# The first product of a squared-ReLU MLP in matmuls of 256 columns, added in PSUM, and a shift of the token tiles

## The chip, the cores and the metric

The kernel runs on one core of a Trainium2 chip. The metric is the device time of one execution in microseconds (us), as the median of several runs. A profile of one execution gives the times of single instructions; it names the engines PE (TensorE, the matmuls), PEld (TensorE's weight loads), ACT (ScalarE), DVE (VectorE), POOL (GpSimd) and SP (SyncE, which issues the loads). "L521" is line 521 of the kernel that the profile belongs to.

## The reference

A trunk of two layers on 256 tokens of 2048 floats. The first layer mixes tokens by a convolution module, the second by latent attention; each is followed by an MLP of width 8192, and a norm stands ahead of every part. The MLP is the part that matters here:

```python
def sq_relu_mlp(h, w1, w2):
    return jnp.square(jax.nn.relu(h @ w1)) @ w2

for layer in range(DEPTH):
    ...
    h = rms_norm(x, norm_mlp_g[layer])
    x = x + sq_relu_mlp(h, mlp_w1[layer], mlp_w2[layer])
return rms_norm(x, final_norm_g)
```

Here x is 256 x 2048, w1 2048 x 8192 and w2 8192 x 2048, all in float32.

## The kernel before, in words

**Products in three terms.** TensorE multiplies in a rounded format (float32r). A float32 matrix `a` is therefore split into `hi` (rounded) and `lo` (the rest), and a product `a b` is taken as hi·hi + hi·lo + lo·hi. ScalarE writes `hi` and VectorE the difference `lo` (`split_into`, lines 431 and 432). In down products `mm3` (L200 to L202) issues the three matmuls, each of 512 columns.

**Tokens.** The normed tokens stand transposed in four tiles `xt`, made by `open_xt`. Each holds four of the 16 slices k of 128 input channels; a slice is 256 floats `xh` (hi of the 256 tokens), and right behind it 256 floats `xl` (lo). `xhl(k)` takes both as one operand of 512 columns. The tiles are written by transposes on TensorE (L256, `to_T`), by `residual_stage` for what follows.

**The first product of the MLP**, `h @ w1`, is cut into up units of 128 of the 8192 inner channels: a load of 1 MB of w1 and two chunks of eight slices. The weights are the stationary operand, the tokens stream. Chunk 0 issues eight matmuls of hi weights on `xhl` (512 columns: hi·hi in the left half of the PSUM tile, hi·lo in the right half; L521), then eight of low weights on `xh` (256 columns into the left half; L519); chunk 1 the low ones first. So a unit is 16 wide and 16 narrow matmuls, into one PSUM tile of 512 columns, which ScalarE copies into the tile `U` (L526). Of every two units, `add` puts the two halves together on VectorE (L538), `square` takes the maximum with 0 and the square on ScalarE (L543, then L546 or L549), `forms` (from L555) and `part` (L431, L432) make the operands of the second product. These steps wait in the list `todo`, and `stream` takes one or two of them whenever it prepares a chunk's weights, six chunks (`WB`) ahead of the chunk that TensorE runs.

**The second product** is cut into down units, each for a 1 MB piece of w2. In the first three quarters seven of eight use a scheme of seven instead of eight products (S) and one is plain (O), in the last fewer use it; either ends in matmuls of 512 columns from `mm3`.

**Order.** `mlp` goes through four quarters of the inner channels. First come the 16 up units of the first quarter; from then on the up units of the next quarter (T) and the down units of the present one alternate, by the strings of `ORDERS` (L57), and the last quarter's down units end the MLP. With the T that opens the first string, the first 17 up units of a layer follow each other; the other 47 stand in 42 rows of one or two, each row behind a down unit's wide matmuls.

**Other users of the same tiles and lines.** The conv layer (L864 to L866) and two projections in attention (L1453 to L1455, L1476 to L1478) issue their three terms as three matmuls of 256 columns. The conv layer uses `xt` with the tokens' places as they are given by `PAD_XT`. The low weights of up units stand 56 floats into a tile that `LO_GAP` makes 64 floats wider.

Of the kernel before, what the change touches and what calls it, by code (L numbers as in the profile page):

```python
# [10 lines left out]
F32 = mybir.dt.float32  # L11
# [4 lines left out]
ALU = mybir.AluOpType  # L16
# [23 lines left out]
PAD_RIGHT = 40  # L40
LO_GAP = 64
PAD_XT = 16
PAD_KV = 48
# [13 lines left out]
ORDERS = "STSTSTOSTSTSTSTT", "TSTSTSTOSTSTSTST"  # L57
N_S, N_G = 9, 2
SEVENS = tuple(((0, 1, 3, 4, 5, 6, 7),) * 3 + (last,) for last in ((0, 2, 4), (0, 2)))
# [28 lines left out]
def trunk_kernel(  # L88
# [230 lines left out]

    def open_xt(name, pad=0):  # L320
        pool = right_pool(name, 1)
        xt[:] = [
            pool.tile([P, KC // NNB, 2 * S], F32R, name=nm("xt")) for _ in range(NNB)
        ]
        if pad:
            pool.tile([P, pad], F32, name=nm("pad_xt"))

    xhl = lambda k: xt[k // 4][:, k % 4, :]
    xh = lambda k: xhl(k)[:, :S]
    xl = lambda k: xhl(k)[:, S:]  # L330
    open_xt("xtc", PAD_XT)
    spare = []
# [3 lines left out]

    def residual_stage(last, gain, r_scale=None):


        ssq = small.tile([P, T, NNB], F32, tag="ssq", name=nm("ssq"), bufs=2) if last else None  # L340

        def add(n, ps, t):
            sl = slice(n * NB, (n + 1) * NB)
            if r_scale is None:
                nc.vector.tensor_tensor(xs[:, t, sl], ps[t], xs[:, t, sl], op=ALU.add)
            else:
                nc.vector.scalar_tensor_tensor(
                    out=xs[:, t, sl], in0=ps[t], scalar=r_scale[:, t : t + 1], in1=xs[:, t, sl],
                    op0=ALU.mult, op1=ALU.add,
                )  # L350

        def prepare(n, only=None):
            sl = slice(n * NB, (n + 1) * NB)
            if last:
                if gain is not None:
                    for j in range(2):
                        to_T(xs, 4 * n + 2 * j, xh, xl, gain)
                for t in range(T) if only is None else [only]:
                    nc.scalar.activation(spare[-1](), xs[:, t, sl], AF.Square, accum_out=ssq[:, t, n : n + 1])

        return ssq, add, prepare
# [62 lines left out]

    def hi_lo(n, at=0):
        hi = wpool.tile([P, n, NB], F32R, tag="hi", name=nm("hi"), bufs=WB)
        lo = wpool.tile([P, n * NB + LO_GAP], F32R, tag="lo", name=nm("lo"), bufs=WB)
        return [hi, lo[:, at : at + n * NB].rearrange("p (a b) -> p a b", b=NB)]

# [55 lines left out]
    def mlp(layer, ssq, next_gain, finish=None, before=None, last_w1=None):  # L485
# [5 lines left out]
        def u_tile():  # L491
            return first_tiles.pop("u", None) or mp.tile([P, 2, 2 * S], F32, tag="U", name=nm("U"), bufs=2)

# [3 lines left out]
        def up_units(hs, q, p, extra):  # L497
# [5 lines left out]
            def up_unit(b):  # L503
                ps = []

                def chunk(h):
                    def prep(raw, parts):
                        parts[h] = [a.rearrange("p a (j n) -> p (a j) n", n=P) for a in hi_lo(2, LO_GAP - 8)]
                        split_into(parts[h], raw[:, 8 * h : 8 * h + 8, :])

                    def run(parts):
                        if not ps:
                            ps.append(acc_tile())
                        wh, wl = parts.pop(h)
                        for low in (h, 1 - h):
                            for j in range(8):
                                k = 8 * h + j
                                if low:
                                    nc.tensor.matmul(ps[0][:, :S], wl[:, j, :], xh(k), start=False, stop=False)  # L519
                                else:  # L520
                                    nc.tensor.matmul(ps[0], wh[:, j, :], xhl(k), start=k == 0, stop=k == KC - 1)  # L521

                    def out():
                        if b == 0:
                            held["u"] = u_tile()
                        nc.scalar.activation(held["u"][:, b, :], ps[0], AF.Copy)  # L526

                    if h == 0:
                        return Chunk(prep, run)
                    return Chunk(prep, run, [add, lambda: None, square, forms, part] + extra if b == 1 else [], now=out)  # L530

# [3 lines left out]

            def add():
                v = held["u"][:, :, :S]
                nc.vector.tensor_tensor(v, v, held["u"][:, :, S:], op=ALU.add)  # L538

            def square():  # L540
                n_s[0] += large
                v = held["u"][:, :, :S]
                nc.scalar.activation(v, v, AF.Relu)  # L543
                if p in sevens:
# [26 lines left out]
        def down_units(hs, q, n2, held, final):  # L571
# [5 lines left out]
            if last and not made_stage:  # L577
                made_stage.append(residual_stage(True, next_gain, r2))
            nssq, _, prepare = made_stage[0] if last else (None, None, None)
# [703 lines left out]

    ssq, due = mlp(0, ssq, g_mix[1])


    with ExitStack() as cx:
# [447 lines left out]

        open_xt("xt1")
        ssq, add, prepare = residual_stage(True, g_mlp[1])
        for b in range(2):
# [82 lines left out]
```

## Time and profile before

| | |
|---|---|
| timed runs | 1928.03 us median of 3 (1927.92 to 1928.38) |
| profiled execution, from the first to the last instruction | 1926.2 us, about 1.8 us less than the median |
| mean granted TensorE clock | 0.999 |
| instructions | 28463, of which 10768 matmuls |
| read from HBM, written | 363.68 MB, 2.10 MB (190 GB/s over the span) |
| up units, first MLP | from about 314 us on, mixed with down units from 403 us on |
| up units, second MLP | from about 1245 us on, mixed from 1334 us on |

How to read it: busy time of an engine is the sum of its instructions without their overlaps. Since matmuls are pipelined, the duration of one (0.28 us for 256 columns) is longer than the distance to the next one's start, and it is this distance that adds up. A row of a group ends with the mean duration in ns, then the idle time of the engine just ahead of these instructions and what ended most of it. A row of the timeline has start, duration, engine, line, operation, out<-in, shape and number; x8 is eight in a row. A row of the chain has start, duration and what ran.

### The profile page before, as it was taken

The page shows a single profiled execution, that of the slowest core. Times are in us where ns is not written, and L with a number is a line of the kernel's source. Part 1 is how long each engine was busy: PE and PEld are TensorE (multiplying, and loading weights), DVE is VectorE, ACT ScalarE, POOL GpSimd, SP SyncE. Part 2 cuts the span into 40 slices and gives each one's busy share as a digit, 9 for nine tenths or more (in the row PEclk, how much of TensorE's full clock was granted, in tenths as well). Part 3 has the DMA queues.
Part 4 walks back from the last instruction along what each step waited for, and adds up shares of the span by engine and source line. Part 5 has one row for each costly group of instructions (what it writes and reads, how often), then busy time and mean ns, then how long its engine had stood idle before and what let it go on. Part 6 is the DMA issues. An engine that isn't in the chain of part 4 may idle for free.

```text
span 1926.2 us, 28463 instructions
## 1 busy us (share of the span) xinstructions
PE 1900.7 (99%) x10768; PEld 1665.0 (86%) x10768; DVE 1648.4 (86%) x2370; ACT 1206.5 (63%) x1716; POOL 224.6 (12%) x185
## 2 busy tenths in 40 slices
PE   7999999999999999999999999999999999999998
PEld 7999888888888888888899998888888888888886
DVE  5999866789999999999976665667999999999887
ACT  5556754766666666666566665566666666666654
POOL 5999300000000000000001410000000000000000
PEclk9999999999999999999999999999999999999999
DMA  8676456857666677666646445765667666666663
GB/s 236 188 194 180 139 191 160 234 174 209 206 198 201 193 210 211 200 204 204 207 150 180 117 145 178 208 183 175 198 196 212 204 197 198 217 203 196 212 220 109
DMA packets 407114, 367.62 MB, mean 191 GB/s; under 512 B 15417, under 2 KB 351937, under 8 KB 406721
## 3 DMA queue, kind: packets, MB, share of 16 engines
q1 hardware_dynamic: 405952, 363.63, 63.1%
q10 hardware_dynamic: 1024, 2.17, 0.3%
q8 instruction: 84, 1.38, 0.3%
q14 instruction: 54, 0.43, 0.1%
HBM read 363.68 MB, written 2.10 MB: 190 GB/s over the span
## 4 chain that ended last, share of the span: by engine, by line
PE 88%; DVE 8%; ACT 2%; POOL 1%; issue 1%; DMA 1%; DVEq 0%; ACTq 0%; POOLq 0%
PE acc L521 24%; PE acc L201 15%; PE acc L200 15%; PE acc L202 15%; PE acc L519 12%; DVE sum L979 6%; POOL lo L175 1%; PE acc L256 1%; ACT hi L174 1%; PE acc L866 0%; PE acc L865 0%; PE acc L864 0%; PE acc L1589 0%; DMA xs<-in_x 0%; PE acc L1453 0%
## 5 line engine op out<-in xcount | busy, mean ns | idle before, releaser
L432 DVE TENSOR_TENSOR lo<-raw,hi 128x1024 fp32r<-128x1024 f32 (+1 forms) x512 | 570.6, 1121 | 88.1 <-ACT hi L431 87.8
L431 ACT ACTIVATE hi<-raw 128x1024 fp32r<-128x1024 f32 (+1 forms) x512 | 479.6, 970 | 66.3 <-PE acc L201 66.0
L521 PE MATMUL acc<-xt,hi 128*128 128x512 f32 x2048 | 504.3, 391 | 0.0
L521 PEld LDWEIGHTS acc<-xt,hi 128*128 128x128 f32 x2048 | 374.8, 188 | 73.0 <-ACT hi L431 0.4
L200 PE MATMUL acc<-hi,sh 128*128 128x512 f32 x930 | 362.8, 390 | 0.0
L202 PE MATMUL acc<-lo,sh 128*128 128x512 f32 x930 | 361.9, 389 | 0.0
L201 PE MATMUL acc<-hi,sl 128*128 128x512 f32 x802 | 312.0, 389 | 0.0
L519 PEld LDWEIGHTS acc<-xt,lo 128*128 128x128 f32 x2048 | 257.7, 188 | 10.9
L519 PE MATMUL acc<-xt,lo 128*128 128x256 f32 x2048 | 259.7, 279 | 0.0
L174 ACT ACTIVATE hi<-raw 128x1024 fp32r<-128x1024 f32 (+2 forms) x184 | 179.9, 1006 | 47.2 <-PE acc L201 43.0
L202 PEld LDWEIGHTS acc<-lo,sh 128*128 128x128 f32 x930 | 174.6, 188 | 36.3
L200 PEld LDWEIGHTS acc<-hi,sh 128*128 128x128 f32 x930 | 174.6, 188 | 36.0
L175 DVE TENSOR_TENSOR lo<-raw,hi 128x1024 fp32r<-128x1024 f32 (+2 forms) x118 | 132.8, 1145 | 68.6 <-ACT hi L174 62.5
L431 ACT ACTIVATE hi<-V 128x1024 fp32r<-128x1024 f32 x94 | 99.5, 1059 | 130.1 <-DVE V L727 117.4
L201 PEld LDWEIGHTS acc<-hi,sl 128*128 128x128 f32 x802 | 150.5, 188 | 31.2
L979 DVE SCALAR_TENSOR_TENSOR sum<-ub,w_dw,sum 128x256 f32<-128x256 f32 x392 | 158.9, 480 | 6.4 <-ACT sum L935 5.4
L175 POOL TENSOR_TENSOR lo<-raw,hi 128x1024 fp32r<-128x1024 f32 x66 | 157.6, 2406 | 23.1 <-ACT hi L174 22.5
L431 ACT ACTIVATE hi<-T 128x1024 fp32r<-128x1024 f32 x94 | 99.3, 1056 | 92.3 <-DVE T L715 70.5
L526 ACT ACTIVATE U<-acc 128x512 f32<-128x512 f32 x128 | 75.8, 592 | 110.4 <-PE acc L521 110.4
L864 PE MATMUL acc<-xt,hi 128*128 128x256 f32 x512 | 143.5, 280 | 0.0
L866 PE MATMUL acc<-xt,lo 128*128 128x256 f32 x512 | 142.2, 278 | 0.5 <-POOL lo L175 0.5
L865 PE MATMUL acc<-xt,hi 128*128 128x256 f32 x512 | 142.2, 278 | 0.2 <-DVE xt L213 0.2
(275 smaller groups left out, 2800.1 us busy)
## 6 DMA issues: line engine op xcount, KB each, us to landing
raw<-in_mlp_w SPq DMA_DIRECT2D x256, 1024.0 KB, 6.1
raw<-in_conv_w_pw SPq DMA_DIRECT2D x64, 512.0 KB, 5.7
raw<-in_conv_w_pw SPq DMA_DIRECT2D x16, 1024.0 KB, 5.1
raw<-in_mla_w_o SPq DMA_DIRECT2D x16, 1024.0 KB, 5.6
raw<-in_mla_w_kv_up SPq DMA_DIRECT2D x8, 1024.0 KB, 5.2
raw<-in_mla_w_in SPq DMA_DIRECT2D x8, 576.0 KB, 3.8
raw<-in_mla_w_in SPq DMA_DIRECT2D x4, 1024.0 KB, 7.5
raw<-in_mla_w_q_up SPq DMA_DIRECT2D x16, 256.0 KB, 5.0
```

What stands on the lines that cost most here:

```text
L174: nc.scalar.activation(hi, raw[:, js, :], AF.Copy)
L175: eng.tensor_tensor(lo, raw[:, js, :], hi.bitcast(F32), op=ALU.subtract)
L200: nc.tensor.matmul(ps, sh, mh, start=start, stop=False)
L201: nc.tensor.matmul(ps, sl, mh, start=False, stop=False)
L202: nc.tensor.matmul(ps, sh, ml, start=False, stop=stop)
L431: nc.scalar.activation(parts[0], src, AF.Copy)
L432: nc.vector.tensor_tensor(parts[1], src, parts[0].bitcast(F32), op=ALU.subtract)
L519: nc.tensor.matmul(ps[0][:, :S], wl[:, j, :], xh(k), start=False, stop=False)
L521: nc.tensor.matmul(ps[0], wh[:, j, :], xhl(k), start=k == 0, stop=k == KC - 1)
L864: nc.tensor.matmul(o, wh[:, bs], xh(k), start=k == 0, stop=False)
L865: nc.tensor.matmul(o, wh[:, bs], xl(k), start=False, stop=False)
L979: nc.vector.scalar_tensor_tensor(out=out, in0=ubs[c][:, w : w + S], scalar=tap(c, w), in1=pcs[c], op0=ALU.mult, op1=ALU.add)
```

## The change

Matmuls of an up unit: all three terms are 256 columns wide and add in the same 256 columns of PSUM. A chunk issues, for each of its eight slices, hi weights on `xh` and hi weights on `xl` (L517 and L518 of the changed kernel), then eight matmuls of low weights on `xh` (L521); both chunks in this order. A unit has 48 narrow matmuls and 48 weight loads, where it had 16 wide and 16 narrow ones and 32 loads.

Eviction: ScalarE takes the maximum with 0 while it copies 256 columns (L526). The addition on VectorE goes, and so does the separate maximum on ScalarE. `U` is half as large. The list of steps of a pair has a placeholder less: it begins with an empty one, where it began with `add` and an empty one.

Places: a token tile is one flat row of 4 x 512 + 64 floats, and `x_part` takes a slice from a start that can be moved. The start is 48 floats in the conv layer, in both MLPs and for what is written for them, and 0 for attention. The low weights lose their offset and their wider tile.

On TensorE, the place is the first up unit behind a down unit in the first MLP (names: `acc` a PSUM tile, `xt` a token tile, `hi` and `lo` weights, `sh` and `sl` operands made from squares; x4 is four alike in a row). Before, the whole unit with the wide matmul ahead and the one behind:

```order
L202 MATMUL acc_4760<-lo_4657,sh_4028 128x512
L521 MATMUL acc_4781<-xt_3456,hi_4679 128x512 x4
L521 MATMUL acc_4781<-xt_3457,hi_4679 128x512 x4
L519 MATMUL acc_4781<-xt_3456,lo_4680 128x256 x4
L519 MATMUL acc_4781<-xt_3457,lo_4680 128x256 x4
L519 MATMUL acc_4781<-xt_3458,lo_4702 128x256 x4
L519 MATMUL acc_4781<-xt_3459,lo_4702 128x256 x4
L521 MATMUL acc_4781<-xt_3458,hi_4701 128x512 x4
L521 MATMUL acc_4781<-xt_3459,hi_4701 128x512 x4
L200 MATMUL acc_4710<-hi_4719,sh_4128 128x512
```

The unit begins and ends wide, and its only narrow matmuls stand in its middle. After the change, the end of the same unit (its last two slices of hi weights, the low weights, and the next down unit):

```order
L517 MATMUL acc_5020<-xt_3458,hi_4945 128x256
L518 MATMUL acc_5020<-xt_3458,hi_4945 128x256
L517 MATMUL acc_5020<-xt_3458,hi_4945 128x256
L518 MATMUL acc_5020<-xt_3458,hi_4945 128x256
L521 MATMUL acc_5020<-xt_3457,lo_4946 128x256 x4
L521 MATMUL acc_5020<-xt_3458,lo_4946 128x256 x4
L201 MATMUL acc_4954<-hi_4961,sh_4195 128x512
```

The unit now ends narrow, with the low weights of chunk 1 behind its hi weights; its start is alike, with L517 and L518 in turn straight behind the wide L203 of the down unit ahead (the lines of `mm3` are one higher in the changed kernel).

On ScalarE, the place is a pair of up units in the first quarter of the first MLP (names: `U` the evicted pair, `W` its squares, `raw` loaded weights). Before:

```order
L526 ACTIVATE U_4346<-acc_4304 128x512
L431 ACTIVATE hi_4351<-raw_4159 128x1024
L431 ACTIVATE sh_4324<-W_4322 128x896
L431 ACTIVATE hi_4376<-raw_4206 128x1024
L526 ACTIVATE U_4346<-acc_4357 128x512
L431 ACTIVATE hi_4398<-raw_4206 128x1024
L543 ACTIVATE U_4346<-U_4346 128x2x256
L546 ACTIVATE W_4422<-U_4346 128x512
```

After the change:

```order
L526 ACTIVATE U_4481<-acc_4424 128x256
L431 ACTIVATE hi_4486<-raw_4234 128x1024
L431 ACTIVATE sh_4451<-W_4449 128x896
L431 ACTIVATE hi_4519<-raw_4296 128x1024
L526 ACTIVATE U_4481<-acc_4492 128x256
L431 ACTIVATE hi_4548<-raw_4296 128x1024
L541 ACTIVATE W_4579<-U_4481 128x512
```

The two evictions are half as wide, the separate maximum is gone, and the rest stands in the same order.

The diff:

```diff
--- before.py
+++ after.py
@@ -38,8 +38,9 @@
 PAD_VECS = 16
 PAD_SMALL = 8
 PAD_RIGHT = 40
-LO_GAP = 64
-PAD_XT = 16
+XT_PAD = 64
+XT_CONV = 48
+XT_ATT = 0
 PAD_KV = 48
 PAD_STATS = 48
 PAD_O = 16
@@ -55,7 +56,7 @@
 LAST_REST = (20, 16, 0)
 FILL_AT = (5, 15)
 ORDERS = "STSTSTOSTSTSTSTT", "TSTSTSTOSTSTSTST"
-N_S, N_G = 9, 2
+N_S, N_G, N_U = 9, 2, 2
 SEVENS = tuple(((0, 1, 3, 4, 5, 6, 7),) * 3 + (last,) for last in ((0, 2, 4), (0, 2)))
 MADE = tuple((range(8),) * 3 + (last,) for last in ((0, 2, 1, 3, 4, 5, 6, 7),) * 2)
 LATE_G = ((3, 5, 6, 7), (3, 4, 5, 6, 7))
@@ -317,24 +318,25 @@
 
     ctx.callback(lambda: xt_cx[0].close())
 
-    def open_xt(name, pad=0):
+    xt_at = [XT_CONV]
+
+    def open_xt(name):
         pool = right_pool(name, 1)
-        xt[:] = [
-            pool.tile([P, KC // NNB, 2 * S], F32R, name=nm("xt")) for _ in range(NNB)
-        ]
-        if pad:
-            pool.tile([P, pad], F32, name=nm("pad_xt"))
-
-    xhl = lambda k: xt[k // 4][:, k % 4, :]
-    xh = lambda k: xhl(k)[:, :S]
-    xl = lambda k: xhl(k)[:, S:]
-    open_xt("xtc", PAD_XT)
+        xt[:] = [pool.tile([P, KC // NNB * 2 * S + XT_PAD], F32R, name=nm("xt")) for _ in range(NNB)]
+
+    def x_part(k, low, at=None):
+        start = (xt_at[0] if at is None else at) + (2 * (k % 4) + low) * S
+        return xt[k // 4][:, start : start + S]
+
+    xh = lambda k: x_part(k, 0)
+    xl = lambda k: x_part(k, 1)
+    open_xt("xtc")
     spare = []
 
     xh_kt = lambda k, t: xh(k)[:, t * P : (t + 1) * P]
     xl_kt = lambda k, t: xl(k)[:, t * P : (t + 1) * P]
 
-    def residual_stage(last, gain, r_scale=None):
+    def residual_stage(last, gain, r_scale=None, at=None):
 
 
         ssq = small.tile([P, T, NNB], F32, tag="ssq", name=nm("ssq"), bufs=2) if last else None
@@ -354,7 +356,7 @@
             if last:
                 if gain is not None:
                     for j in range(2):
-                        to_T(xs, 4 * n + 2 * j, xh, xl, gain)
+                        to_T(xs, 4 * n + 2 * j, lambda k: x_part(k, 0, at), lambda k: x_part(k, 1, at), gain)
                 for t in range(T) if only is None else [only]:
                     nc.scalar.activation(spare[-1](), xs[:, t, sl], AF.Square, accum_out=ssq[:, t, n : n + 1])
 
@@ -422,10 +424,8 @@
         def __init__(self, prep, run, after=(), now=None, ahead=None):
             self.prep, self.run, self.after, self.now, self.ahead = prep, run, after, now, ahead
 
-    def hi_lo(n, at=0):
-        hi = wpool.tile([P, n, NB], F32R, tag="hi", name=nm("hi"), bufs=WB)
-        lo = wpool.tile([P, n * NB + LO_GAP], F32R, tag="lo", name=nm("lo"), bufs=WB)
-        return [hi, lo[:, at : at + n * NB].rearrange("p (a b) -> p a b", b=NB)]
+    def hi_lo(n):
+        return [wpool.tile([P, n, NB], F32R, tag=c, name=nm(c), bufs=WB) for c in ("hi", "lo")]
 
     def split_into(parts, src):
         nc.scalar.activation(parts[0], src, AF.Copy)
@@ -489,7 +489,7 @@
         made_stage, pre, first_tiles, blocked, n_s, sums_left = [], [], {}, {}, [0], []
 
         def u_tile():
-            return first_tiles.pop("u", None) or mp.tile([P, 2, 2 * S], F32, tag="U", name=nm("U"), bufs=2)
+            return first_tiles.pop("u", None) or mp.tile([P, 2, S], F32, tag="U", name=nm("U"), bufs=N_U)
 
         def f_tile():
             return first_tiles.pop("f", None) or mp.tile([P, 8, P], F32, tag="W", name=nm("W"), bufs=1)
@@ -505,42 +505,37 @@
 
                 def chunk(h):
                     def prep(raw, parts):
-                        parts[h] = [a.rearrange("p a (j n) -> p (a j) n", n=P) for a in hi_lo(2, LO_GAP - 8)]
+                        parts[h] = [a.rearrange("p a (j n) -> p (a j) n", n=P) for a in hi_lo(2)]
                         split_into(parts[h], raw[:, 8 * h : 8 * h + 8, :])
 
                     def run(parts):
                         if not ps:
-                            ps.append(acc_tile())
+                            ps.append(acc_tile()[:, :S])
                         wh, wl = parts.pop(h)
-                        for low in (h, 1 - h):
-                            for j in range(8):
-                                k = 8 * h + j
-                                if low:
-                                    nc.tensor.matmul(ps[0][:, :S], wl[:, j, :], xh(k), start=False, stop=False)
-                                else:
-                                    nc.tensor.matmul(ps[0], wh[:, j, :], xhl(k), start=k == 0, stop=k == KC - 1)
+                        for j in range(8):
+                            k = 8 * h + j
+                            nc.tensor.matmul(ps[0], wh[:, j, :], xh(k), start=k == 0, stop=False)
+                            nc.tensor.matmul(ps[0], wh[:, j, :], xl(k), start=False, stop=False)
+                        for j in range(8):
+                            k = 8 * h + j
+                            nc.tensor.matmul(ps[0], wl[:, j, :], xh(k), start=False, stop=k == KC - 1)
 
                     def out():
                         if b == 0:
                             held["u"] = u_tile()
-                        nc.scalar.activation(held["u"][:, b, :], ps[0], AF.Copy)
+                        nc.scalar.activation(held["u"][:, b, :], ps[0], AF.Relu)
 
                     if h == 0:
                         return Chunk(prep, run)
-                    return Chunk(prep, run, [add, lambda: None, square, forms, part] + extra if b == 1 else [], now=out)
+                    return Chunk(prep, run, [lambda: None, square, forms, part] + extra if b == 1 else [], now=out)
 
                 unit = Unit(rows(w1, 0, KC, ((q * NPAIR + p) * 2 + b) * P, P), KC, [chunk(h) for h in range(2)])
                 unit.last_read = 1
                 return unit
 
-            def add():
-                v = held["u"][:, :, :S]
-                nc.vector.tensor_tensor(v, v, held["u"][:, :, S:], op=ALU.add)
-
             def square():
                 n_s[0] += large
-                v = held["u"][:, :, :S]
-                nc.scalar.activation(v, v, AF.Relu)
+                v = held["u"]
                 if p in sevens:
                     held["f"] = f = f_tile()
                     nc.scalar.activation(f[:, 0:4, :].rearrange("p (b t) n -> p b (t n)", b=2), v, AF.Square)
@@ -575,7 +570,7 @@
             last_plain = max(p for p in range(NPAIR) if p not in sevens)
             last = q == PARTS - 1
             if last and not made_stage:
-                made_stage.append(residual_stage(True, next_gain, r2))
+                made_stage.append(residual_stage(True, next_gain, r2, XT_ATT))
             nssq, _, prepare = made_stage[0] if last else (None, None, None)
             na, nb = 2 * n2, 2 * n2 + 1
             ends = (1, nb), (1, na), (0, nb), (0, na)
@@ -1282,6 +1277,7 @@
         nc.scalar.activation(cos, an2, AF.Sin)
 
     ssq, due = mlp(0, ssq, g_mix[1])
+    xt_at[0] = XT_ATT
 
 
     with ExitStack() as cx:
@@ -1734,6 +1730,7 @@
             prefetch()
 
         open_xt("xt1")
+        xt_at[0] = XT_CONV
         ssq, add, prepare = residual_stage(True, g_mlp[1])
         for b in range(2):
             for t in range(T):
```

## Prediction

> **What bounds the kernel now.** I read the page first, then TensorE's windows over the two MLPs, then the chain of work, and last the single matmuls in the timeline. The page gives the shares:
>
> ```profile
> span 1926.2 us, 28463 instructions
> PE 1900.7 (99%) x10768; PEld 1665.0 (86%) x10768; DVE 1648.4 (86%) x2370; ACT 1206.5 (63%) x1716; POOL 224.6 (12%) x185
> PE 88%; DVE 8%; ACT 2%; POOL 1%; issue 1%; DMA 1%; DVEq 0%; ACTq 0%; POOLq 0%
> L521 PE MATMUL acc<-xt,hi 128*128 128x512 f32 x2048 | 504.3, 391 | 0.0
> L521 PEld LDWEIGHTS acc<-xt,hi 128*128 128x128 f32 x2048 | 374.8, 188 | 73.0 <-ACT hi L431 0.4
> L519 PE MATMUL acc<-xt,lo 128*128 128x256 f32 x2048 | 259.7, 279 | 0.0
> ```
>
> The span is 1926.2 us; the median of the timed runs is 1928.03, so about 1.8 us lie around the span. TensorE is busy 99% of it. In the last three rows the number behind the second bar is idle time: none ahead of the matmuls of L521 and L519, the two lines that the change replaces. The weight loads of L521 show 73.0 us of idle time, of which 0.4 waited for ScalarE; a load runs beside the matmul ahead of it, so that idle time costs nothing. The windows of the first MLP (first its up units alone, then those mixed with down units) say the same; the columns are busy time, number, granted clock, DMA share, GB/s:
>
> ```profile
> 313.60:402.80 89.20, 89.20 (x519) 1.00 0.67 185
> 402.80:810.00 407.20, 407.20 (x2093) 1.00 0.67 201
> ```
>
> Here TensorE is busy every microsecond at clock 1.00. So the time of this stage is the number of matmuls times the distance from one start to the next, and the change counts only as far as it moves that distance. The chain gives it for the up units (start, duration, matmuls in a row):
>
> ```profile
> 340.62 3.66 PE acc L521 x16
> 346.15 3.66 PE acc L521 x16
> ...
> 377.44 1.87 PE acc L519 x16
> 379.31 3.66 PE acc L521 x16
> ```
>
> An up unit takes 5.53 us (346.15 - 340.62): 16 matmuls of 512 columns in 3.66 and 16 of 256 in 1.87, so 228.8 and 116.9 ns each. The same unit between down products, in the timeline (start, duration; the last matmul's end overlaps what follows, so I use starts):
>
> ```profile
> 401.25 2.00 PE L521 MATMUL acc<-xt,hi 128*128 128x512 f32 x8
> 403.10 0.39 PE L200 MATMUL acc<-hi,sh 128*128 128x512 f32 x1
> ...
> 407.63 0.39 PE L202 MATMUL acc<-lo,sh 128*128 128x512 f32 x1
> 407.86 1.98 PE L521 MATMUL acc<-xt,hi 128*128 128x512 f32 x8
> 409.68 2.03 PE L519 MATMUL acc<-xt,lo 128*128 128x256 f32 x16
> 411.54 2.00 PE L521 MATMUL acc<-xt,hi 128*128 128x512 f32 x8
> 413.38 0.39 PE L200 MATMUL acc<-hi,sh 128*128 128x512 f32 x1
> ```
>
> 413.38 - 407.86 is 5.52 us. Settled wide matmuls stand at (407.63 - 403.10)/20 = 226.5 ns. Eight of them take 1.82 us from 407.86, but 1.85 from 401.25 and 1.84 from 411.54: entering wide matmuls from narrow ones costs about 0.03 us, once in each unit.
>
> **The change: matmuls.** Each of 128 up units (64 per layer) now issues 48 matmuls of 256 columns instead of 16 wide and 16 narrow. The columns are the same, 48 x 256. So what counts is the distance of narrow matmuls, against 5527/48 = 115.1 ns on average now. The trace has long rows of matmuls of exactly the new form (256 columns, one load of 128x128 each, hi and low weights on the token tiles xt) in the conv layer. They come in two paces. Three windows of 10 us there:
>
> ```profile
> 63.00:73.00 10.00, 10.00 (x91) 1.00 0.77 208
> 74.20:84.20 10.00, 10.00 (x87) 1.00 0.76 208
> 85.40:95.40 10.00, 10.00 (x91) 1.00 0.76 206
> ```
>
> Equal clock, no idle time, nearly equal DMA, and yet 91 matmuls against 87 (each count has two or three that reach over the edges). From starts the faster pace is:
>
> ```profile
> 64.11 0.28 PE L864 MATMUL acc<-xt,hi 128*128 128x256 f32 x1
> ...
> 70.91 0.28 PE L864 MATMUL acc<-xt,hi 128*128 128x256 f32 x1
> ```
>
> There are 60 steps in 6.80 us: 113.3 ns, half of a wide one. Call this the fast pace. The slow one I take from the one place where such matmuls follow straight behind wide products, in the attention layer:
>
> ```profile
> 1035.81 0.39 PE L201 MATMUL acc<-hi,xt 128*128 128x512 f32 x1
> 1036.03 0.39 PE L202 MATMUL acc<-lo,xt 128*128 128x512 f32 x1
> 1036.26 0.28 PE L1453 MATMUL acc<-kvh,hi 128*128 128x256 f32 x1
> 1036.38 0.28 PE L1454 MATMUL acc<-kvl,hi 128*128 128x256 f32 x1
> ...
> 1038.97 0.28 PE L1455 MATMUL acc<-kvh,lo 128*128 128x256 f32 x1
> ```
>
> From 1036.26 to 1038.97 stand 23 steps in 2.71 us: 117.8 ns, from the first step to the last, with no drift to the other pace. In the conv layer, where a row of 96 begins behind two transposes, 5 of the 14 long rows between 62 and 198 us keep the slow pace, 9 the fast one (every third is slow, as in the three windows). So a row takes its pace at its start and keeps it. In one place it changed, at a change of tiles:
>
> ```profile
> 1051.15 0.28 PE L202 MATMUL acc<-lo,qh 128*128 128x256 f32 x1
> 1051.27 0.29 PE L1476 MATMUL acc<-qh,hi 128*128 128x256 f32 x1
> ...
> 1053.89 0.28 PE L1478 MATMUL acc<-qh,lo 128*128 128x256 f32 x1
> ```
>
> Here 23 steps take 2.62 us, 113.9 on average: the fast pace again, behind narrow matmuls. At up units behind down products what stands ahead is wide, as at 1036.03. Of the 128 units, 94 stand in 84 rows entered from a wide down product (L200 to L202); the other 34 are the first 17 units of each layer, behind transposes. I take the attention row for the 94: 48 x 117.8 = 5.654 us against 5.527, **+0.127 x 94 = +11.9 us**. The bound below is 48 x 113.3 = 5.440, -0.087 each, -8.2. For the 34 the conv rows hold: the fast pace gives -3.0, the slow one +4.3; with 5 of 14 slow that is **-0.4**. At 86 places a narrow row now ends in wide products and these settle in 0.03 us (1.85 against 1.82 above): 86 x 0.027 = **+2.3**. In the old units this transition is inside the 5.527; the new units have none inside.
>
> **The tokens' place.** By the addresses of the two programs, the shift puts the MLP's tokens where the conv layer's and kv's stand, counted modulo 256 bytes (0, with all weights at 64; before 64, with low weights at 32); so the rows of conv and kv are the nearest ones for the new units. The conv layer and the attention projections keep their tokens where they were. The wide down products read neither, and I leave them at 226.5.
>
> The Trainium skill, "TensorE: Matmul & The Clock Gate", section "Step-by-step: what each phase is for", says that TensorE has two ports into SBUF, so that loading the next weights takes nothing from the running matmul. By that alone all narrow rows would keep 113.3 ns and the change would be worth what the first rival says; the trace has the same form at 117.8 too, without idle time and at clock 1.00, so something that the rule leaves out sets the pace.
>
> **Weight loads.** They rise from 32 to 48 per unit, at 188 ns each as before. A load beside every 256 columns is what the conv rows have, so its price is inside 113.3 to 117.8, and there is no extra term.
>
> **ScalarE and VectorE.** Rows of what goes and of the nearest eviction with 256 columns:
>
> ```profile
> L526 ACT ACTIVATE U<-acc 128x512 f32<-128x512 f32 x128 | 75.8, 592 | 110.4 <-PE acc L521 110.4
> L538 DVE TENSOR_TENSOR U<-U 128x512 f32<-128x512 f32 x64 | 44.1, 688 | 21.9 <-ACT U L526 20.4
> L543 ACT ACTIVATE U<-U 128x512 f32<-128x512 f32 x64 | 40.0, 625 | 9.4 <-DVE U L538 9.4
> L206 ACT ACTIVATE kTh<-acc 128x256 fp32r<-128x256 f32 x16 | 6.3, 392 | 2.2 <-PE acc L1455 2.1
> ```
>
> ScalarE loses L543's 40.0 us and 128 x (592 - 392) = 25.6; VectorE loses 44.1. None of it is on the path: TensorE waits at most 0.4 us for them (L521's row), so I take 0, with 0.4 as the gain's bound. No wait is added; the eviction still follows the unit's last matmul, and weights are still made three units ahead. Later steps of a pair come sooner, and their consumers are down products a quarter later.
>
> **The conv layer** keeps its addresses, but its start could shift the rows' paces. VectorE covers it:
>
> ```profile
> 57.00:180.00 123.00, 123.00 (x1074) 123.00 (x1073) 122.48 (x315) 70.49 (x113) 120.30 (x77) 1.00 0.69 189
> ```
>
> The columns are PE, PEld, DVE, ACT, POOL: VectorE is at 122.48 of 123.00, too. I count 0; without that cover, a row of 96 that changes pace is worth 96 x 4.5 ns = 0.4 us, and 14 rows at most 6.
>
> **Sum**: 11.9 - 0.4 + 2.3 = +13.8 us on the profiled 1926.2 + 1.8 = 1928.0: **1942 us**.
>
> **Rivals.** *First, the fast pace everywhere.* TensorE takes 113.3 ns behind wide products as well: 128 x -0.087 + 2.3 = -8.8, **1919 us**. For it speak 9 of 14 conv rows and the change at 1051.27; against it the only entry from wide products. It turns to the other side where fewer than 41 of the 128 units are slow: each slow unit costs 0.214 more than a fast one, and 8.8/0.214 = 41.
>
> *Second, the slow pace everywhere*, start rows as well: 128 x 0.127 + 2.3 = +18.6, **1947 us**. For it: five conv rows begin so behind transposes; against it nine that don't.
>
> *Third, mixed rows*: pace by pace as the down products happen to end, half of the 94 slow: +1.9 - 0.4 + 2.3 = +3.8, **1932 us**. Against it: a row's predecessors are alike at all 84 entries (matmuls of 512 columns at 226.5 ns), and one cause should give one pace.
>
> *Fourth, the spared evictions and additions pay* (that they are what the change really brings): at most 0.4 us by the row of L521, so this alters no case by more than that.
>
> **How the numbers follow.** The forecast (slow behind wide products, start rows either way: 1939 to 1947 with the second rival at its end) has 0.66, the second rival 0.08, the mixed one 0.09, the fast one 0.17. A measurement of this kernel tells about 0.2% (3.9 us) from no change. The mixed case lies around that edge: 0.05 of its 0.09 within, 0.04 slower. That makes faster 0.17, same 0.05, slower 0.78. The range has to leave out no more than 0.2: it leaves out the fast rival and what of the mixed case lies below, and reaches from 1930 to 1949 (the second rival, with some of conv's 6 us).
>
> **What would show it.** In the changed profile, an up unit among down products takes 5.65 us from its first start to the next L201, and its windows show TensorE without idle time. A unit of the first quarter takes 5.44 or 5.65. Wide products behind a unit take 1.85 us for the first eight. The forecast is wrong if units among down products stand at 5.44, if TensorE shows idle time in the MLP, or if the wide products leave 226.5 ns.

## The result and the profile after

The changed kernel took 1942.76 us (median of four runs: 1938.29, 1941.19, 1944.34, 1944.55), the kernel before 1928.16: a ratio of 1.0072, with a 95% interval of 1.0058 to 1.0087, so slower by 0.7%. The forecast was 1942. One execution of number 2 (3894.71 us) and one of number 8 (2377.75 us, granted clock 0.753) were far slower than the rest and enter no ratio below. The profiled execution has a span of 1942.6 us, 16.4 more than before. The page of the changed kernel answers to the rows shown of before:

```profile
span 1942.6 us, 32430 instructions
PE 1916.7 (99%) x12816; PEld 1765.6 (91%) x12816; DVE 1609.7 (83%) x2306; ACT 1147.9 (59%) x1652; POOL 224.6 (12%) x185
L517 PE MATMUL acc<-xt,hi 128*128 128x256 f32 x2048 | 494.3, 281 | 0.0
L518 PE MATMUL acc<-xt,hi 128*128 128x256 f32 x2048 | 494.2, 281 | 0.0
L521 PE MATMUL acc<-xt,lo 128*128 128x256 f32 x2048 | 282.9, 281 | 0.0
L526 ACT ACTIVATE U<-acc 128x256 f32<-128x256 f32 x128 | 49.1, 383 | 206.8 <-PE acc L521 206.7
```

TensorE is still the bound, with no idle time ahead of the three lines. ScalarE and VectorE are less busy (59% and 83%, before 63% and 86%), the eviction takes 383 ns instead of 592 and stands idle longer for TensorE: the relief is there, and nobody was waiting for it. TensorE's timeline at one up unit between down products, and at three in a row:

```profile
409.55 0.39 PE L203 MATMUL acc<-lo,sh 128*128 128x512 f32 x1
409.77 0.28 PE L517 MATMUL acc<-xt,hi 128*128 128x256 f32 x1
409.89 0.28 PE L518 MATMUL acc<-xt,hi 128*128 128x256 f32 x1
410.01 0.28 PE L517 MATMUL acc<-xt,hi 128*128 128x256 f32 x1
...
415.43 0.39 PE L201 MATMUL acc<-hi,sh 128*128 128x512 f32 x1
417.24 0.39 PE L203 MATMUL acc<-lo,sh 128*128 128x512 f32 x1
...
477.69 0.28 PE L517 MATMUL acc<-xt,hi 128*128 128x256 f32 x1
494.65 0.39 PE L201 MATMUL acc<-hi,sh 128*128 128x512 f32 x1
```

A unit takes (494.65 - 477.69)/3 = 5.653 us, 117.8 ns for a matmul: the slow pace, from the first step behind L203 on. It is so in each of the 84 rows behind down products. (By the trace 78 of these rows have one unit and six have three, 96 units in all, and each start row has 16; the description of the kernel and the prediction have rows of one or two, 94 units and 17.) Behind the unit, the first eight wide matmuls take 417.24 - 415.43 = 1.81 us, so the way back costs nothing. The rows of the first quarters (start rows from here on), in windows of 10 us (the count behind x holds two or three matmuls over the edges, so 87 or 88 is the slow pace, 90 or 91 the fast one):

```profile
370.00:380.00 10.00, 10.00 (x87) 1.00 0.68 203
1300.00:1310.00 10.00, 10.00 (x88) 1.00 0.67 187
```

Both start rows are slow in this execution. So all 128 units have the slow pace: 128 x (5.653 - 5.53) = 15.7 of the 16.4 us. Of these the 84 rows hold about 12.1 and the two start rows, 90.07 us each against 88.34 and 88.07 before, 3.7.

### The profile page after: what moved, and what is told of

Same layout as the page of the kernel before. It is cut to its first block, busy times and chain, and to the rows that moved or that the text cites. A ratio compares the mean times of both kernels' runs of the same rounds, so it can differ in the third digit from the quotient of the medians.

```text
span 1942.6 us, 32430 instructions
## 1 busy us (share of the span) xinstructions
PE 1916.7 (99%) x12816; PEld 1765.6 (91%) x12816; DVE 1609.7 (83%) x2306; ACT 1147.9 (59%) x1652; POOL 224.6 (12%) x185
## 4 chain that ended last, share of the span: by engine, by line
PE 88%; DVE 7%; ACT 2%; POOL 1%; DMA 1%; issue 1%; DVEq 0%; POOLq 0%; ACTq 0%
PE acc L201 15%; PE acc L202 15%; PE acc L203 15%; PE acc L517 12%; PE acc L518 12%; PE acc L521 12%; DVE sum L974 6%; POOL lo L176 1%; PE acc L257 1%; ACT hi L175 1%; PE acc L861 0%; PE acc L860 0%; PE acc L859 0%; PE acc L1585 0%; DMA xs<-in_x 0%
## 5 line engine op out<-in xcount | busy, mean ns | idle before, releaser
L431 ACT ACTIVATE hi<-raw 128x1024 fp32r<-128x1024 f32 (+1 forms) x512 | 484.7, 973 | 85.4 <-PE acc L202 83.8
L517 PE MATMUL acc<-xt,hi 128*128 128x256 f32 x2048 | 494.3, 281 | 0.0
L518 PE MATMUL acc<-xt,hi 128*128 128x256 f32 x2048 | 494.2, 281 | 0.0
L517 PEld LDWEIGHTS acc<-xt,hi 128*128 128x128 f32 x2048 | 387.7, 189 | 3.3
L518 PEld LDWEIGHTS acc<-xt,hi 128*128 128x128 f32 x2048 | 386.7, 189 | 3.3
L203 PE MATMUL acc<-lo,sh 128*128 128x512 f32 x930 | 362.0, 389 | 0.0
L521 PE MATMUL acc<-xt,lo 128*128 128x256 f32 x2048 | 282.9, 281 | 0.0
L521 PEld LDWEIGHTS acc<-xt,lo 128*128 128x128 f32 x2048 | 259.9, 189 | 0.0
L203 PEld LDWEIGHTS acc<-lo,sh 128*128 128x128 f32 x930 | 174.6, 188 | 36.2
L526 ACT ACTIVATE U<-acc 128x256 f32<-128x256 f32 x128 | 49.1, 383 | 206.8 <-PE acc L521 206.7
L859 PE MATMUL acc<-xt,hi 128*128 128x256 f32 x512 | 143.5, 280 | 0.0
L861 PE MATMUL acc<-xt,lo 128*128 128x256 f32 x512 | 142.2, 278 | 0.5 <-POOL lo L176 0.5
```

Source lines behind the costliest of these rows:

```text
L203: nc.tensor.matmul(ps, sh, ml, start=False, stop=stop)
L431: nc.scalar.activation(parts[0], src, AF.Copy)
L517: nc.tensor.matmul(ps[0], wh[:, j, :], xh(k), start=k == 0, stop=False)
L518: nc.tensor.matmul(ps[0], wh[:, j, :], xl(k), start=False, stop=False)
L521: nc.tensor.matmul(ps[0], wl[:, j, :], xh(k), start=False, stop=k == KC - 1)
L859: nc.tensor.matmul(o, wh[:, bs], xh(k), start=k == 0, stop=False)
```

## The experiments

Three theories go through them. *Entry*: a row of narrow matmuls has one of two paces, and what stands ahead of the row picks it. *Place*: the place of tokens and weights in their tiles sets the pace. *Load*: the distance of narrow matmuls is that of their weight loads, whatever the columns (against *stream*, the columns). Times of before in the same comparisons were 1927.8 to 1928.1 us.

**1. The places alone.** The old wide matmuls, eviction, addition and maximum, at the new places (an excerpt: the loops around the matmuls and the side work are left out):

```diff
+nc.tensor.matmul(ps[0][:, :S], wl[:, j, :], xh(k), ...)
+nc.tensor.matmul(ps[0], wh[:, j, :], xhl(k), ...)
-nc.tensor.matmul(ps[0], wh[:, j, :], xh(k), ...)
-nc.tensor.matmul(ps[0], wh[:, j, :], xl(k), ...)
-nc.tensor.matmul(ps[0], wl[:, j, :], xh(k), ...)
```

> The shift of the tokens (and of the low weights) alone, with the old matmuls of 512 and 256 columns, the old eviction, addition and maximum. Theory 'entry' (a row of narrow matmuls has one of two paces, 113.3 or 117.8 ns, and takes the slow one behind wide products): L521's wide matmuls keep 226.7 ns; the 16 low-weight matmuls of a unit, between wide ones, go from 116.9 to 113.3 or 117.8 ns, so a unit goes from 5.53 to between 5.47 and 5.55 us and the kernel to between 1921 and 1930 us. Theory 'place' (the new places by themselves make TensorE slower): most of the 14.6 us show up here, 1938 us or more.

1932.77 us, ratio 1.0025 (1.0015 to 1.0034). Its timeline at a unit between down products:

```profile
407.97 2.03 PE L525 MATMUL acc<-xt,hi 128*128 128x512 f32 x8
409.84 1.99 PE L523 MATMUL acc<-xt,lo 128*128 128x256 f32 x16
411.66 2.02 PE L525 MATMUL acc<-xt,hi 128*128 128x512 f32 x8
413.52 0.40 PE L201 MATMUL acc<-hi,sh 128*128 128x512 f32 x1
```

The 16 narrow ones got faster (1.82 us, 113.8 ns, before 1.86), but eight wide ones take 1.87 and 1.86 us instead of 1.82 and 1.84. *Entry* had said that wide matmuls on the moved tokens keep their pace; they don't, the moved places cost wide matmuls time. *Place* had said that most of the 14.6 us show up here; it is 4.8. So neither theory's number came out.

**2. The narrow matmuls alone.** The kernel before with the new matmuls and eviction; `LO_GAP`, `PAD_XT` and the tokens' places as before.

> The narrow matmuls and the new eviction alone; tokens and low weights stay at the places of before. Theory 'entry': the width of what stands ahead decides, and the places matter little: 5.65 us for a unit between down products, 1938 to 1945 us. Theory 'place': hi-weight matmuls keep half of a wide one's pace (113.3) and low-weight ones the 116.9 ns of L519 in before, 32 x 113.3 + 16 x 116.9 = 5.50 us for a unit, about 1925 us.

1952.6 us, ratio 1.0126 (1.0111 to 1.0142): 24.6 us lost.

```profile
410.75 0.28 PE L517 MATMUL acc<-xt,hi 128*128 128x256 f32 x1
410.87 0.28 PE L518 MATMUL acc<-xt,hi 128*128 128x256 f32 x1
...
416.46 0.40 PE L200 MATMUL acc<-hi,sh 128*128 128x512 f32 x1
418.29 0.39 PE L202 MATMUL acc<-lo,sh 128*128 128x512 f32 x1
```

A unit takes 5.71 us (119 ns), a pace of its own, and the eight wide ones behind it 1.83. All its rows have it, the start rows too. *Entry* without the place is refuted, and so is *place* as it was stated (5.50 us for a unit). The two halves of the change don't add up: the shift costs 4.8 us under wide matmuls and gives back about 10 under narrow ones.

**3. Shorter weight loads.** 112 weight columns in 47 of a unit's 48 matmuls (the rest of the channels gets one term only); one of the three lines, the others are alike:

```diff
-nc.tensor.matmul(ps[0], wl[:, j, :], xh(k), ...)
+nc.tensor.matmul(ps[0][:112], wl[:, j, :112], xh(k), ...)
```

> The changed kernel with 112 instead of 128 weight columns in 47 of the 48 matmuls of an up unit (16 of 128 inner channels of a unit get one term only). Theory 'load' (the next weight load is what a narrow row waits for): the load gets shorter, the pace falls below 113.3 ns everywhere, toward 107 to 110, and the kernel to 1880 to 1905 us. Theory 'stream' (256 columns of tokens, whatever the weights): the pace stays 117.8, 1938 to 1945 us.

1961.28 us in a single run, outside both expectations. The first start of a unit and the first wide one behind it, then the loads of one line (189 ns each in the changed kernel):

```profile
411.49 0.28 PE L519 MATMUL acc<-xt,hi 128*128 128x256 f32 x1
...
417.25 0.39 PE L202 MATMUL acc<-hi,sh 128*128 128x512 f32 x1
```

```profile
L520 PEld LDWEIGHTS acc<-xt,hi 128*112 128x112 f32 x2048 | 364.0, 178 | 3.3
```

A load takes 178 ns, yet a unit takes 5.76 us, 120.0 ns for a matmul. Fewer weight columns made it slower; that speaks against *stream* (117.8 expected), but not for *load* as stated. The Trainium skill, "TensorE: Matmul & The Clock Gate", section "Weight-path perf modes — Fast Weight Load (FWL) and DoubleRow", says that a faster load is on when the number of weights is 128 and the input type is not FP32; the weights here are float32r, and whether that rule reaches them and is the reason here, no run shows. The run settles nothing, and number 7 asks again.

**4. Another entry.** Outside the first quarter, the first matmul of each unit is cut into two of 128 columns:

```diff
-nc.tensor.matmul(ps[0], wh[:, j, :], xh(k), start=k == 0, stop=False)
+if k == 0 and q > 0:
+    for s in (0, P):
+        nc.tensor.matmul(ps[0][:, s : s + P], wh[:, j, :], xh(k)[:, s : s + P], start=s == 0, stop=False)
+else: ...
```

> The changed kernel; in all units but those of the first quarter the first matmul is cut into two of 128 columns, so that a row enters with another spacing. Theory 'entry': some or all of the 84 rows behind down products come out at the fast pace, 5.44 us for a unit; if all do, 94 x 0.21 = 20 us less than the changed kernel, 1918 to 1926 us with the price of the extra matmuls. Theory 'place': the pace stays 117.8 ns, and the extra 96 matmuls make it 1940 to 1947 us.

1933.62 us, ratio 1.0032 (1.0019 to 1.0044), 9 us less than the changed kernel, with 96 matmuls more.

```profile
409.91 0.33 PE L519 MATMUL acc<-xt,hi 128*128 128x128 f32 x2
410.08 0.33 PE L522 MATMUL acc<-xt,hi 128*128 128x256 f32 x1
410.25 0.28 PE L521 MATMUL acc<-xt,hi 128*128 128x256 f32 x1
410.37 0.28 PE L522 MATMUL acc<-xt,hi 128*128 128x256 f32 x1
...
415.47 0.39 PE L201 MATMUL acc<-hi,sh 128*128 128x512 f32 x1
```

From 410.25 on the rest of the unit, 46 matmuls, takes 5.22 us: 113.5 ns. All 84 rows changed to the fast pace by this one cut, at equal places: *entry* is shown, for these places. The cut has a price: the first three matmuls take 0.34 us (410.25 - 409.91), where two of 256 columns took 0.23. The columns are the same, with one whole load more; that pointed to *load* again. In 96 units these 0.11 us make 10.6, which is why the time lies above the expected 1918 to 1926.

**5 and 6. Other places.** `XT_CONV = 32` and `XT_CONV = 16` instead of 48, nothing else.

> The changed kernel with the tokens 32 instead of 48 floats into their tiles (conv layer and both MLPs). Theory 'entry' by itself (only what stands ahead picks between 113.3 and 117.8 ns, places don't): 5.65 us for a unit between down products, 1938 to 1945 us, as in the changed kernel. Theory 'entry and place' (the run at the old places had 118.9 ns in all rows, also in the start rows, so the place sets which paces exist): another pace than 117.8 ns; at the old places' 118.9 the kernel takes about 1952 us, at 113.3 about 1919.

> The same with the tokens 16 floats into their tiles. Theory 'entry' by itself: 1938 to 1945 us. Theory 'entry and place': another pace than 117.8 ns, between 1919 us (113.3 ns everywhere) and 1955 us (119 ns everywhere).

1965.01 us (1.0192, 1.0177 to 1.0207) and 1949.01 us (1.0110, 1.0095 to 1.0125). In the run with 32, then in the one with 16, the first matmul of a unit, the first wide one behind it, and the ninth:

```profile
416.04 0.28 PE L517 MATMUL acc<-xt,hi 128*128 128x256 f32 x1
...
421.79 0.39 PE L201 MATMUL acc<-hi,sh 128*128 128x512 f32 x1
...
423.65 0.39 PE L203 MATMUL acc<-lo,sh 128*128 128x512 f32 x1
```

```profile
413.84 0.28 PE L517 MATMUL acc<-xt,hi 128*128 128x256 f32 x1
...
419.50 0.40 PE L201 MATMUL acc<-hi,sh 128*128 128x512 f32 x1
...
421.35 0.39 PE L203 MATMUL acc<-lo,sh 128*128 128x512 f32 x1
```

Units of 5.75 us (119.8 ns) and 5.66 (117.9), and about 1.85 us in both for the eight wide matmuls behind, where the changed kernel has 1.81. So with 32 the place gives another pace, as *entry and place* expected. With 16 it doesn't: behind down products the pace is the changed kernel's, and the second start row is fast throughout (113.3 ns), so both of its paces exist here too. The longer time of number 6 comes from the way back (0.04 us at 84 rows, 3 us) and from the conv layer, whose tokens move too: the first up unit starts at 318.13 us with 16 and at 319.37 with 32, and at 313.82 in the changed kernel. That part belongs to neither expectation. The changed kernel's 48 takes the least time of the four placings tried.

**7. Half of the columns.** Low weights on 128 of the 256 tokens (the term is left out for the others):

```diff
-nc.tensor.matmul(ps[0], wl[:, j, :], xh(k), ...)
+nc.tensor.matmul(ps[0][:, :P], wl[:, j, :], xh(k)[:, :P], ...)
```

> The changed kernel with low weights on 128 of the 256 tokens, so that a third of the up units' matmuls has half of its columns (the low-weight term is left out for the other half of the tokens). Theory 'load' (behind a narrow matmul the next one waits for its own weight load, whatever the columns; two halves in the run with a split first matmul took one whole load more): the 128-column matmuls keep 113 to 118 ns, the kernel 1930 to 1945 us. Theory 'stream' (columns set the distance): they take 57 to 60 ns, a unit 5.65 - 16 x 0.058 = 4.7 us, the kernel about 1825 us.

1925.78 us in a single run, below what *load* expected. A chunk's last hi matmul, its eight low ones and what follows, up to the next eight:

```profile
408.44 0.28 PE L518 MATMUL acc<-xt,hi 128*128 128x256 f32 x1
408.56 1.01 PE L521 MATMUL acc<-xt,lo 128*128 128x128 f32 x8
409.40 0.33 PE L517 MATMUL acc<-xt,hi 128*128 128x256 f32 x1
409.57 0.28 PE L518 MATMUL acc<-xt,hi 128*128 128x256 f32 x1
...
410.05 0.28 PE L518 MATMUL acc<-xt,hi 128*128 128x256 f32 x1
...
411.29 1.01 PE L521 MATMUL acc<-xt,lo 128*128 128x128 f32 x8
```

Eight matmuls of 128 columns take 0.84 us. The second starts at 408.62, 0.06 us behind the first, about what 128 columns would take at half of 113.3 ns; the other seven take (0.84 - 0.06)/7 = 0.11 us each, 112 ns in the trace. Another 0.05 is paid at the first matmul behind them (0.17 us to the next one). A third of the matmuls lost half of its columns and the kernel 17 us, where *stream* gave 117: *stream* is refuted below 256 columns. *Load* fits: the first half finds the next weights loaded during the long matmul ahead, the others don't. It is not shown to be the cause, since every matmul here has its own load (12816 of each), so another cost paid once per matmul would look alike. Nor does it follow that loads set the pace at 256 columns: the fast 113.3 ns are just half of a wide matmul's 226.5.

The Trainium skill, "TensorE: Matmul & The Clock Gate", section "LDWEIGHTS (loading the stationary operand)", gives a load in ns as its columns divided by 1.2, so 107 for 128. The distance of 112 here is near that; the profile's own duration of a load, 189 ns, is longer, and the 120.0 of number 3, with 112 columns, go the other way.

The halves also change the pace: the unit enters at 118 ns, and from 410.05 on eleven matmuls of 256 columns take 411.29 - 410.05 = 1.24 us, 113 ns each.

**8. Wide products in halves.** The last wide matmul of each down unit is issued as two of 256 columns, so that a row enters from narrow ones (an excerpt; the calls that ask for halves are left out):

```diff
-nc.tensor.matmul(ps, sh, ml, start=False, stop=stop)
+for s in (0, S) if halves else (None,):
+    cols = slice(None) if s is None else slice(s, s + S)
+    nc.tensor.matmul(ps[:, cols], sh, ml[:, cols], start=False, stop=stop and s != 0)
```

> The changed kernel; the last wide matmul of every down unit is cut into two of 256 columns, so that an up unit enters from narrow matmuls and not from a wide one; 128 more matmuls. Theory 'entry': the rows' pace can change, to 113.3 ns in some or all of the 84 rows; if in all, 94 x 0.21 = 20 us less than the changed kernel plus 2.3 us for the way back to wide ones, 1921 to 1928 us. Theory 'place': 117.8 ns stays, 1939 to 1947 us.

1928.8 us, ratio 0.9998 (0.9988 to 1.0007): 14 us less than the changed kernel, level with the one before, and just above the expected 1921 to 1928.

```profile
409.94 0.40 PE L205 MATMUL acc<-lo,sh 128*128 128x256 f32 x2
410.17 0.29 PE L519 MATMUL acc<-xt,hi 128*128 128x256 f32 x1
410.29 0.28 PE L520 MATMUL acc<-xt,hi 128*128 128x256 f32 x1
...
415.63 0.39 PE L201 MATMUL acc<-hi,sh 128*128 128x512 f32 x1
...
417.46 0.39 PE L205 MATMUL acc<-lo,sh 128*128 128x512 f32 x1
```

The two halves take 0.23 us, as the wide one did, and the unit 5.46: the fast pace in all 84 rows, nearly for nothing. Its runs stand at 1925.7 to 1925.9 or at 1928.8 to 1929.2 us: a start row is 16 units, and 16 x (5.653 - 5.44) = 3.4 us lie between its paces. The same step is in number 4 (1933.6 or 1936.8) and in the changed kernel's runs (1938.3, 1941.2, 1944.4). The profiled executions bear it out: number 8's (1925.7) has one start row of 90.07 us and one of 86.69, those of number 4 (1936.8) and of the changed kernel (1944.3) have both at 90.07. That the other steps are two, one or none of the start rows fast is inferred from the times.

**9. The start rows too.** Number 8, and two cuts as in number 4 at the second and third unit of each first quarter.

> The run with wide products in halves, and in the first quarter the first matmul of the second and third unit cut into two of 128 columns, as a second and third chance for the start rows to leave the slow pace. Theory 'entry': a cut gives another spacing, the two start rows end in 113.3 ns, and the kernel takes 1922 to 1924 us in all runs (3 us less for each start row that was slow, 0.5 us for four more loads). Rival: once in a row, the slow pace can't be left inside narrow matmuls; then 1926 to 1929.5 us, as the run with halves alone.

**1923.0 us, ratio 0.9976 (0.9967 to 0.9985): faster than both kernels**, by 5 us against before. Two of its eleven runs lie above the expected 1922 to 1924. The profiled execution was the slowest (1923.9 us from the first to the last instruction, 1925.67 with what lies around it), and shows the first start row being cut at 320.43 and 325.99 us:

```profile
320.43 0.33 PE L521 MATMUL acc<-xt,hi 128*128 128x128 f32 x2
...
325.99 0.33 PE L521 MATMUL acc<-xt,hi 128*128 128x128 f32 x2
...
331.55 0.38 PE L523 MATMUL acc<-xt,hi 128*128 128x256 f32 x1
331.77 0.28 PE L524 MATMUL acc<-xt,hi 128*128 128x256 f32 x1
```

Between the cuts, 49 matmuls take 5.56 us, as in number 4: the first cut brought the row from the slow to the fast pace. At 331.55 a matmul stands 0.22 us ahead of the next, and behind this pause the row is slow again to its end. So a row does not always keep the pace that it entered with: a pause can change it. It need not: in the first start row of number 6 a unit that begins late, at 335.46, turns the row from fast to slow, and in that of number 10 one at 332.74 leaves it fast.

**10. The spared work put back.** Eviction by copy, an operation of 128x512 on VectorE in the place of the addition, and the separate maximum (an excerpt):

```diff
-nc.scalar.activation(held["u"][:, b, :], ps[0], AF.Relu)
+nc.scalar.activation(held["u"][:, b, :], ps[0], AF.Copy)
+nc.vector.tensor_tensor(v, v, v, op=ALU.max)
+nc.scalar.activation(v, v, AF.Relu)
```

> The changed kernel with the old side work put back: the eviction copies, VectorE has an operation of 128x512 where the addition was (a maximum of the tile with itself), and ScalarE the separate maximum. If the spared work is off the path, as forecast: the time of the changed kernel, 1938 to 1945 us, each unit between down products 5.65 us. Rival (the spared work of 40 + 44 us gave something back that hid more cost): 1948 us or more.

1940.43 us, ratio 1.0062 (1.0047 to 1.0078), its four runs from 1937.8 to 1944.4, the changed kernel's range. Its two operations, and its start rows in the same windows as above:

```profile
L538 DVE TENSOR_TENSOR U<-U 128x512 f32<-128x512 f32 x64 | 44.1, 689 | 28.2 <-ACT U L526 27.7
L543 ACT ACTIVATE U<-U 128x512 f32<-128x512 f32 x64 | 39.9, 623 | 6.7 <-DVE U L538 6.5
```

```profile
370.00:380.00 10.00, 10.00 (x90) 1.00 0.69 204
1300.00:1310.00 10.00, 10.00 (x87) 1.00 0.63 173
```

84 us of work on two engines moved nothing that can be told from the start rows' steps. In the mixed stage of the first MLP, behind the start row, it can be told exactly: from the first wide matmul behind the start row to the first behind the last up unit the changed kernel takes 908.93 - 405.02 = 503.9 us, and this run 907.51 - 403.58 = 503.9. And here the first start row is fast and the second slow, in a kernel whose matmuls are those of the changed one.

**11. Halves at the old places.** Number 2 with the halves of number 8.

> Narrow matmuls with tokens and low weights at the places of before, and the last wide product of each down unit in halves. If entry alone decides (narrow matmuls ahead bring the fast pace): 113.3 ns behind down products, 5.46 us for a unit, 1928 to 1936 us. If the place sets which paces exist and entry only picks among them: about 118.9 ns stays, 5.70 us for a unit, 1951 to 1955 us.

1955.3 us, ratio 1.0141 (1.0124 to 1.0158).

```profile
410.56 0.40 PE L204 MATMUL acc<-lo,sh 128*128 128x256 f32 x2
410.79 0.28 PE L519 MATMUL acc<-xt,hi 128*128 128x256 f32 x1
...
416.50 0.40 PE L200 MATMUL acc<-hi,sh 128*128 128x512 f32 x1
```

A unit keeps 5.71 us. The same entry that flips every row at the new places does nothing at the old ones: the places (tokens and low weights together) set which paces exist, entry picks among them.

## Why the prediction was right, point by point

- **TensorE alone counts**: right, with no idle time after the change; and the 84 us of spared side work are worth nothing (number 10).
- **Slow pace behind wide products** (+11.9 us for 94 units): right in mechanism and size, 5.653 us for a unit against 5.654 forecast, in all 84 rows; numbers 4 and 8 show that the entry is the cause, since they alter it alone and get 113.5 to 113.8 ns. The count was 96 units instead of 94, which makes the term 12.2.
- **Start rows** (-0.4 us, by the conv layer's share of slow rows): they are no fixed mix. A start row comes out slow or fast from one execution to the next, 3.4 us each; the profiled execution had both slow, +3.7 measured. The conv share was misread as well: of the twelve rows of 96 matmuls there four are slow, not 5 of 14, in both kernels; that moves the term by 0.2 us only.
- **The way back to wide matmuls** (+2.3 us): this term failed. It was measured behind narrow matmuls of the old places (L519 to L521), and it is nothing behind slow rows of the new ones (1.81 us for eight wide, where 1.85 was forecast), 0.02 to 0.04 elsewhere (numbers 2, 5, 6 and 8). With it out, all rows slow come to 1928.0 + 11.9 + 4.3 = 1944.2 by the prediction's own prices; the profiled execution's 1942.6 + 1.8 is 1944.4.
- **The total** (1942 against 1942.76): that it is so near is partly luck. The two terms above were wrong and made +1.9 together, and the median of the four runs is the middle between 1941.2 and 1944.3, two draws of the start rows. The direction and most of the size rest on the 84 rows and are no luck.
- **The conv layer** (0, because VectorE covers it): 0 was right, since its rows kept their paces, but the cover isn't there. In number 6 all twelve rows are slow, and the stage ends 4.3 us later.
- **The rows that were taken as nearest**: choosing rows of equal places was the step that mattered. At the old places the same matmuls lose 24.6 us.
- **Weight loads** ("no extra term"): right as a sum, for the rows that were read held it already. Behind narrower matmuls the price shows: at 128 columns, 112 ns a matmul (number 7). Whether loads make the slow pace at 256 columns, no run shows; at the fast one they cost nothing beside the columns (2 x 113.3 against 226.5 ns).
- **First rival** (1919 us, fast pace everywhere): not what the change does, but the state can be had: number 9 comes to 1923.0, with what remains in entries (5.46 instead of 5.44 us for a unit), the way back and, in the profiled execution, a start row that a pause turned slow.

What stays open: why a row holds one of two paces, why a pause changes it in one case and not in another, and why the place in a tile decides which exist. The runs show that it does so, with equal clock and no idle time; what in the chip makes it was not measured.

## What to carry to other kernels

Where TensorE is busy without a gap, cost a matmul by the distance of starts in rows of the same width, with the same places of both operands and the same predecessor, and not by its columns. Two matmuls of 256 columns took as long as one of 512 at the fast pace only; at the others each took 4 to 7 ns more, by the place and the entry, and that adds up over thousands of them. When runs of one kernel differ by equal steps, look for rows that can come out at two paces.

## What the runs showed of the hardware that was not expected

- Matmuls of 128 columns, each with its own load, take 112 ns one behind the other, hardly less than those of 256 (113.3 to 119.8 by place and entry); 512 take 226.5.
- The place of the tokens decides which paces a narrow row can have: 48 and 16 floats into the tile gave 113.3 and 117.8 ns, 32 gave 118.8 to 119.8, and the old places 119.
- One matmul cut in two, or one wide matmul issued in halves, changes the pace of the whole row behind it (117.8 to 113.3 ns), and a pause of 0.22 us in a fast row turned it slow.
- 112 instead of 128 weight columns made the matmuls slower, 120.0 against 117.8 ns.
